# A hybrid decoder layer: the low weights of gate and up 64 bytes further in their tile, the mixers' later tiles realigned, a diagonal moved into a token tile

## The chip, the cores and the metric

One core of a Trainium2 chip runs the whole layer as one program. The metric is the device time of one execution in microseconds (us). The kernel before takes 1016.15 us (median of three runs, 1015.79 to 1016.25).

## The reference

All values are float32, the sequence has 256 tokens, the model width D is 2048, the feed-forward width 5632.

```python
h = rms_norm(x, g_mix)
z_pool, z_q, z_kv, z_kr, z_mq = split(h @ w_in)
y = concat(pool_mixer(z_pool), mla_mixer(z_q, z_kv, z_kr), memory_cross_attention(z_mq, mem))
x = x + y @ w_o
h = rms_norm(x, g_ffn)
g, u = h @ w_gate, h @ w_up                 # 2048 x 5632 each
gc = conv_b + sum(conv_w[j] * shift(g, j))  # causal, width 3, along tokens
x = x + (silu(gc) * u) @ w_down
```

The weights are streamed once from HBM, about 190 MB, and each is used for 256 tokens.

## The kernel before

**Two parts for each number.** A product is made of rounded fp32 parts (the type is called fp32r). Each loaded weight tile `wr` (128 partitions x 2048 columns) is cut by `split_w` (L92) into a high part `wh`, cast by ScalarE (L98), and a low part `wl`, the difference, by VectorE (L99), 1024 columns at a time. `wr`, `wh` and `wl` have three buffers each. Activations have such a pair too, stored side by side: 256 columns of the high part and 256 of the low part. What is computed is high x high, high weight x low activation and low weight x high activation.

**Two ways round.** TensorE (PE) multiplies a stationary operand, 128x128, which a LDWEIGHTS brings in (PEld in the profile), by a moving operand that is streamed past it.

- `gemm_t` (L103), used for gate, up and the input projections, takes the *weights* as stationary. For eight blocks of 128 input features it issues eight products with `wh`, each moving all 512 columns of the activation (both parts at once), and eight with `wl`, each moving the 256 columns of the high part. The order is high, low, low, high, so that sixteen high products stand in a row, then sixteen low ones. Line L116 is both, told apart by the names `h,wh` and `h,wl` (`h` is `h2`, the normalized input of the feed-forward part) or `xg,wh` and `xg,wl` (the input projections).
- `gemm_n` (L122), used for the latent up-projections, the memory's keys and values and the output projection, takes the *activation* as stationary (`mg`, `xg`, `zl`, `cat`, `catm`) and moves 512 columns of `wh` (L134, L135) and `wl` (L136). The down projection does the same (L832 to L834) with the activations `aT` and `aS`.

**Stages by time in the profile.** Memory keys and values to 51 us, queries and rope keys to 78 us, input projections and latent up-projections (stationary `zl`) to 179 us, the output projection (stationary `cat`, and `catm` for the memory heads, with attention heads between) to 290 us, gate and up to 782 us (44 blocks, for each a gate tile and an up tile of 1 MB), the down projection to the end.

**Where things lie.** SBUF addresses are given out in the order of allocation and are fixed when the program is built. In the program before, `wr`, `wh`, `wl`, `h2`, `mg`, `xg`, `cat` and `aT` all begin 64 bytes past a multiple of 128. `gqk` (L311) is 8 bytes wide, and what the mixers allocate behind it (`rot`, `kr`, `tok`, `catm`, `zl`, `p` and others) begins 96 bytes past a multiple of 128, so 32 bytes off from the rest. The blocks of 128 columns inside these tiles are 512 bytes long, so every stationary block keeps its tile's offset.

**The diagonal.** `x1_rstd` (L739) puts the reciprocal root of the mean square on a diagonal `dg` (L743) and multiplies by ones (L745), which gives it as a row for all partitions, `r1`. `dg` has a constant tile of 1024 bytes. `tok` is a tag with three buffers for short-lived token-major tiles in the mixers' pool, which is released after `x1_rstd`; the feed-forward tiles (`g`, `gc`, `u`, `aT`, `aS`) are then put at the same place.

The order within an engine is mostly decided by a scheduler from priorities and dependences; `keep` fixes it by hand in places.

Of the kernel before, what the change touches and what calls it, by code (L numbers as in the profile page):

```python
# [11 lines left out]
F32 = mybir.dt.float32  # L12
F32R = mybir.dt.float32r
# [5 lines left out]
P = 128  # L19
# [41 lines left out]
def layer(ctx, tc, xT_d, xn_d, memT_d, vec_d, tab_d, w_z_d, w_mqkr_d, w_q_d, w_kv_d, w_mem_d, w_pool_d, w_o_d,  # L61
# [10 lines left out]
    def nm(s):  # L72
        uid[0] += 1
        return f"{s}_{uid[0]}"
# [14 lines left out]

        return tc.keep_in_program_order(ins) if on else ins  # L90

    def split_w(raw, o, n, cut=HS, kept=False):  # L92

        hi = stage.tile([P, HS], F32R, tag="wh", name=nm("wh"), bufs=3)
        lo = stage.tile([P, HS], F32R, tag="wl", name=nm("wl"), bufs=3)
        for c in range(0, n, cut):
            e = min(n, c + cut)
            keep(nc.scalar.copy(hi[:, c:e], raw[:, o + c:o + e]), kept)  # L98
            keep(nc.vector.tensor_tensor(lo[:, c:e], raw[:, o + c:o + e], hi[:, c:e].bitcast(F32), op=ALU.subtract),  # L99
                 kept)  # L100
        return hi, lo

    def gemm_t(ps, raw, o, act, ks, first=True, last=True, kept=False, between=None):  # L103


        ks = list(ks)
        nk = HS // P
        cs = range(0, len(ks), nk)
        for c in cs:
            kc = ks[c:c + nk]  # L110
            hi, lo = split_w(raw, o + c * P, len(kc) * P)

            for low in ((False, True) if c // nk % 2 == 0 else (True, False)):
                for i, k in enumerate(kc):
                    w = (lo if low else hi)[:, i * P:(i + 1) * P]
                    keep(nc.tensor.matmul(ps[:, T if low else 0:2 * T], w, act(k)[:, 0:T] if low else act(k),  # L116
                                          start=first and c + i == 0 and not low,
                                          stop=last and c == cs[-1] and i == len(kc) - 1 and low == (c // nk % 2 == 0),
                                          skip_group_check=True), kept)
            if between is not None and c == 0:  # L120
                between()

    def gemm_n(pss, hi, lo, act, k0, first, last, kept=False):

        nk, n = hi.shape[1], hi.shape[2]
        nj = len(pss[0])
        w = n // nj
        for i in range(nk):
            for tt in range(NT):
                xh = act[:, k0 + i, tt * P:(tt + 1) * P]  # L130
                xl = act[:, k0 + i, T + tt * P:T + (tt + 1) * P]
                for j in range(nj):
                    ps, o = pss[tt][j], slice(j * w, (j + 1) * w)
                    keep(nc.tensor.matmul(ps, xh, hi[:, i, o], start=first and i == 0, stop=False), kept)  # L134
                    keep(nc.tensor.matmul(ps, xl, hi[:, i, o], start=False, stop=False), kept)  # L135
                    keep(nc.tensor.matmul(ps, xh, lo[:, i, o], start=False, stop=last and i == nk - 1), kept)  # L136
# [34 lines left out]
    def rsqrt_(dst, src, scale):  # L171

        nc.scalar.activation(dst, src, AF.Sqrt, bias=eps[:], scale=scale)
        nc.vector.reciprocal(dst, dst)
# [96 lines left out]
    for c in range(KD // 2):  # L271
        raw = raw0 if c == 0 else load_w(w_mem_d[c], STG)
        if 0 < c < KD // 2 - 1:
            nc.sync.dma_start(xT[:, 2 * c + 2:2 * c + 4, :], memT_d[:, 2 * c + 2:2 * c + 4, :])
        for i in range(2):
            k = 2 * c + i
            mem_parts(k, k + 1)
            hi, lo = split_w(raw, i * HS, HS, 512 if c == 0 else HS, True)
            gemm_n(pss, hi[:].unsqueeze(1), lo[:].unsqueeze(1), mg, k, k == 0, k == KD - 1)
        if c % 2:  # L280
            h = slice(2 * c - 2, 2 * c + 2)
            ms.add(xT[:, h, :])
            nc.gpsimd.dma_start(xT[:, h, :], xT_d[:, h, :])
        if c in (4, 6):
            x_parts(2 * c - 8, 2 * c - 4)
# [22 lines left out]
    tab = mp.tile([P, NTAB], F32, name="tab")  # L308
    nc.sync.dma_start(tab[:], tab_d)

    gqk = mp.tile([P, 2], F32, name="gqk")  # L311
    keep(nc.vector.tensor_tensor(gqk[:, 0:1], v("gq_nope"), v("gk_nope"), op=ALU.mult))
    keep(nc.vector.tensor_tensor(gqk[:, 1:2], v("g_q_x"), v("g_k_x"), op=ALU.mult))
    rot = mp.tile([P, 2, NT, 4, 32], F32, name="rot")
# [236 lines left out]
    def q_up(n):  # L551
        raw = load_w(w_q_d[n], STG)
        pss = [[ps_main()[:]] for _ in range(NT)]
        for i in range(2):
            hi, lo = split_w(raw, i * HS, HS)
            gemm_n(pss, hi[:].rearrange("p (k n) -> p k n", n=512), lo[:].rearrange("p (k n) -> p k n", n=512),
                   zl, 2 * i, i == 0, i == 1)
        for tt in range(NT):
            ps = pss[tt][0]
            t = tok()  # L560
            if n < 2:
                nc.scalar.copy(t[:], ps)
                head_sq(ssq_n[:, tt, 4 * n:4 * n + 4], t[:].rearrange("p (h d) -> p h d", d=NOPE))
                to_features(qnT[:, 4 * n:4 * n + 4], t, tt, 4, gqk[:, 0:1])
            else:
                t1 = tok()
                nc.scalar.copy(t1[:], ps)
                p3 = t1[:].rearrange("p (h d) -> p h d", d=ROPE)
                head_sq(ssq_r[:, tt, :], p3)
                rotate(t[:].rearrange("p (h d) -> p h d", d=ROPE), p3, 0, tt, H)  # L570
                to_features(qrT, t, tt, 4)
# [9 lines left out]
    def kv_up(n):  # L581
        raw = load_w(w_kv_d[n], STG)
        for h in range(2):
            pss = [[ps_main()[:]] for _ in range(NT)]
            hi, lo = split_w(raw, h * HS, HS)
            gemm_n(pss, hi[:].rearrange("p (k n) -> p k n", n=512), lo[:].rearrange("p (k n) -> p k n", n=512),
                   zl, 4, True, True)
            for tt in range(NT):
                ps = pss[tt][0]
                p3 = ps.rearrange("p (h d) -> p h d", d=128)  # L590
                if n == 1:
                    nc.scalar.activation(vv[:, tt, 4 * h:4 * h + 4, :], p3, AF.Copy, scale=skv[:, tt:tt + 1])
                    continue
                t = tok()
                t3 = t[:].rearrange("p (h d) -> p h d", d=NOPE)
                o = slice(tt * H + 4 * h, tt * H + 4 * h + 4)
                nc.scalar.copy(t[:], ps)
                head_sq(fk[:, o], t3)
                nc.vector.tensor_scalar(fk[:, o], fk[:, o], skv2[:, tt:tt + 1], sskr[:, tt:tt + 1],
                                        op0=ALU.mult, op1=ALU.add)  # L600
                rsqrt_(fk[:, o], fk[:, o], 1.0 / QK)
                nc.vector.tensor_scalar(fkn[:, o], fk[:, o], skv[:, tt:tt + 1], None, op0=ALU.mult)
                nc.vector.tensor_scalar(fkr[:, o], fk[:, o], rx[:, tt:tt + 1], None, op0=ALU.mult)
                nc.vector.tensor_tensor(t3, t3, fkn[:, o].unsqueeze(2).to_broadcast([P, 4, NOPE]), op=ALU.mult)
                to_features(knT[:, 4 * h:4 * h + 4], t, tt, 4, None, "v")
# [73 lines left out]
    def out_part(i, n, pss, c):  # L679

        raw = load_w(w_o_d[i, n, c], STG)
        for h in range(2):
            hi, lo = split_w(raw, h * HS, HS)
            w = [t[:].rearrange("p (k n) -> p k n", n=NN) for t in (hi, lo)]
            k = c * 4 + h * 2
            act, k = (cat, 4 + k) if i else (cat, k) if k < 4 else (catm, k - 4)
            for r in range(2):
                kept = i == 0 or n + c == 0
                gemm_n(pss, *(t[:, r:r + 1] for t in w), act, k + r, c + h + r == 0, c + h + r == 3, kept)
                if kept:  # L690
                    mla_steps()
# [42 lines left out]

    rc = const.tile([P, NT], F32, name="rc")
    r1 = const.tile([P, T], F32, name="r1")
    dg = const.tile([P, T], F32, name="dg")

    def x1_rstd():  # L739
        nc.vector.tensor_reduce(rc[:], ssx[:], axis=AX.X, op=ALU.add)  # L740
        rsqrt_(rc[:], rc[:], 1.0 / D)
        for tt in range(NT):
            nc.vector.tensor_scalar(dg[:, tt * P:(tt + 1) * P], identf[:], rc[:, tt:tt + 1], None, op0=ALU.mult)  # L743
        ps = ps_aux()
        nc.tensor.matmul(ps[:, 0:T], ones[:], dg[:], start=True, stop=True)  # L745
        nc.scalar.copy(r1[:], ps[:, 0:T])


# [56 lines left out]
    for f in range(1, KF):  # L805
        pss = []
        for w in (w_g_d, w_u_d):
            raw = load_w(w[f], STG)
            pss.append(ps_main())
            gemm_t(pss[-1], raw, 0, lambda k: h2[:, k, :], range(KD))  # L810
        glu(f, *pss)


# [190 lines left out]
```

## Time and profile before

| | |
|---|---|
| median of the runs | 1016.15 us |
| profiled execution, its time | 1015.66 us |
| profiled execution, its span | 1013.9 us |
| granted TensorE clock, mean | 0.999 |
| busy: PE, PEld, DVE, ACT | 99%, 86%, 74%, 57% of the span |
| read from HBM | 195 MB, 197 GB/s over the span |

The span is the time from the first to the last instruction; 1.8 us of the execution's time lies around it. PE is busy nearly throughout, so a group's line in the profile (how many, mean duration of one) says less than the distance between the starts of two products that follow each other, here called the **pitch**. A product's recorded duration contains the way through the array and overlaps the next one's; the pitch is what a row of products costs. It is read from the timeline, where equal instructions that follow each other are merged into a row with their first start and their count.

### The profile page before, as it was taken

The page shows a single profiled execution, that of the slowest core. Times are in us where ns is not written, and L with a number is a line of the kernel's source. Part 1 is how long each engine was busy: PE and PEld are TensorE (multiplying, and loading weights), DVE is VectorE, ACT ScalarE, POOL GpSimd, SP SyncE. Part 2 cuts the span into 40 slices and gives each one's busy share as a digit, 9 for nine tenths or more (in the row PEclk, how much of TensorE's full clock was granted, in tenths as well). Part 3 has the DMA queues.
Part 4 walks back from the last instruction along what each step waited for, and adds up shares of the span by engine and source line. Part 5 has one row for each costly group of instructions (what it writes and reads, how often), then busy time and mean ns, then how long its engine had stood idle before and what let it go on. Part 6 is the DMA issues. An engine that isn't in the chain of part 4 may idle for free.

```text
span 1013.9 us, 14132 instructions
## 1 busy us (share of the span) xinstructions
PE 1008.2 (99%) x5356; PEld 868.6 (86%) x5356; DVE 752.4 (74%) x1134; ACT 577.5 (57%) x853; POOL 18.5 (2%) x39
## 2 busy tenths in 40 slices
PE   9999999999999999999999999999999999999998
PEld 7898888888888888888888888888888888888886
DVE  6878689855677676777767676776767788888886
ACT  6678666544576555555545555554655555545653
POOL 1010000000000000000000000000000000010000
PEclk9999999999999999999999999999999999999999
DMA  9777344344665555555555555555545765575561
GB/s 337 278 252 286 130 162 177 130 143 144 210 206 207 181 193 192 183 201 176 197 180 203 178 196 190 185 187 190 205 170 207 256 217 194 208 284 210 208 208 42
DMA packets 31476, 200.17 MB, mean 197 GB/s; under 512 B 3632, under 2 KB 4144, under 8 KB 9392
## 3 DMA queue, kind: packets, MB, share of 16 engines
q1 hardware_dynamic: 28368, 189.44, 52.8%
q0 software_dynamic: 2752, 9.44, 2.6%
q8 instruction: 42, 0.69, 0.3%
q10 hardware_dynamic: 288, 0.38, 0.1%
q14 instruction: 26, 0.21, 0.1%
HBM read 195.06 MB, written 4.19 MB: 197 GB/s over the span
## 4 chain that ended last, share of the span: by engine, by line
PE 99%; DMA 0%; SPq 0%; DVE 0%; ACT 0%; issue 0%
PE psm L116 54%; PE psm L134 5%; PE psm L136 5%; PE psm L135 5%; PE psm L834 4%; PE psa L834 4%; PE psm L833 4%; PE psa L832 4%; PE psa L833 4%; PE psm L832 4%; PE psa L653 1%; PE psa L134 1%; PE psa L136 1%; PE psa L135 1%; PE psa L232 1%; PE psa L429 1%
## 5 line engine op out<-in xcount | busy, mean ns | idle before, releaser
L99 DVE TENSOR_TENSOR wl<-wr,wh 128x1024 fp32r<-128x1024 f32 (+2 forms) x338 | 392.4, 1165 | 65.4 <-ACT wh L98 59.7
L98 ACT CAST wh<-wr 128x1024 fp32r<-128x1024 f32 (+2 forms) x338 | 338.8, 1004 | 138.3 <-PE psm L135 48.6
L116 PE MATMUL psm<-h,wh 128*128 128x512 f32 x1408 | 336.9, 391 | 0.0
L116 PEld LDWEIGHTS psm<-h,wh 128*128 128x128 f32 x1408 | 258.5, 188 | 49.9
L116 PEld LDWEIGHTS psm<-h,wl 128*128 128x128 f32 x1408 | 180.8, 191 | 7.0
L116 PE MATMUL psm<-h,wl 128*128 128x256 f32 x1408 | 182.9, 283 | 0.0
L99 DVE TENSOR_TENSOR wl<-dn,wh 128x1024 fp32r<-128x1024 f32 x58 | 67.8, 1221 | 26.3 <-ACT wh L98 26.3
L98 ACT CAST wh<-dn 128x1024 fp32r<-128x1024 f32 x58 | 59.2, 1052 | 38.3 <-PE psm L833 21.7
L758 ACT COPY g<-psm 128x256 f32<-128x256 f32 x44 | 16.4, 374 | 91.3 <-PE psm L116 91.2
L759 DVE TENSOR_TENSOR g<-g,psm 128x256 f32<-128x256 f32 x44 | 18.5, 420 | 61.0 <-ACT g L758 61.0
L759 DVE TENSOR_TENSOR u<-u,psm 128x256 f32<-128x256 f32 x44 | 18.5, 421 | 55.6 <-ACT u L758 55.6
L769 ACT ACTIVATE gc<-gc 128x256 f32<-128x256 f32 x44 | 18.4, 418 | 63.8 <-DVE gc L768 63.7
L768 DVE SCALAR_TENSOR_TENSOR gc<-g,vec,gc 128x255 f32<-128x255 f32 x88 | 42.1, 478 | 0.3
L832 PE MATMUL psa<-wh,aT 128*128 128x512 f32 x104 | 40.5, 389 | 0.0
L833 PE MATMUL psa<-wh,aT 128*128 128x512 f32 x104 | 40.5, 389 | 0.0
L834 PE MATMUL psa<-wl,aT 128*128 128x512 f32 x104 | 40.5, 389 | 0.0
L832 PE MATMUL psm<-wh,aT 128*128 128x512 f32 x104 | 40.5, 389 | 0.0
L833 PE MATMUL psm<-wh,aT 128*128 128x512 f32 x104 | 40.5, 389 | 0.0
L834 PE MATMUL psm<-wl,aT 128*128 128x512 f32 x104 | 40.5, 389 | 0.0
L116 PE MATMUL psm<-xg,wh 128*128 128x512 f32 x160 | 40.0, 394 | 0.0
L134 PE MATMUL psm<-wh,cat 128*128 128x512 f32 x96 | 38.2, 398 | 0.0
L136 PE MATMUL psm<-wl,cat 128*128 128x512 f32 x96 | 37.5, 390 | 0.0
(227 smaller groups left out, 1394.6 us busy)
## 6 DMA issues: line engine op xcount, KB each, us to landing
wr<-in_w_g SPq DMA_DIRECT2D x44, 1024.0 KB, 4.8
wr<-in_w_u SPq DMA_DIRECT2D x44, 1024.0 KB, 4.8
wr<-in_w_dn SPq DMA_DIRECT2D x33, 1024.0 KB, 4.8
wr<-in_w_o SPq DMA_DIRECT2D x16, 1024.0 KB, 4.9
dn<-in_w_dn SPq DMA_DIRECT2D x11, 1024.0 KB, 4.8
wr<-in_w_z SPq DMA_DIRECT2D x10, 1024.0 KB, 5.7
wr<-in_w_mem SPq DMA_DIRECT2D x7, 1024.0 KB, 7.9
wr<-in_w_mqkr SPq DMA_DIRECT2D x8, 576.0 KB, 4.1
```

The costliest lines, as they stand in the source:

```text
L98: keep(nc.scalar.copy(hi[:, c:e], raw[:, o + c:o + e]), kept)
L99: keep(nc.vector.tensor_tensor(lo[:, c:e], raw[:, o + c:o + e], hi[:, c:e].bitcast(F32), op=ALU.subtract), kept)
L116: keep(nc.tensor.matmul(ps[:, T if low else 0:2 * T], w, act(k)[:, 0:T] if low else act(k), start=first and c + i == 0 and not low, stop=l ...
L134: keep(nc.tensor.matmul(ps, xh, hi[:, i, o], start=first and i == 0, stop=False), kept)
L135: keep(nc.tensor.matmul(ps, xl, hi[:, i, o], start=False, stop=False), kept)
L136: keep(nc.tensor.matmul(ps, xh, lo[:, i, o], start=False, stop=last and i == nk - 1), kept)
L759: nc.vector.tensor_tensor(t[:], t[:], ps[:, T:2 * T], op=ALU.add)
L768: nc.vector.scalar_tensor_tensor(gc[:, d:T], g[:, 0:T - d], v(w, f), gc[:, d:T], op0=ALU.mult, op1=ALU.add)
L769: nc.scalar.activation(gc[:], gc[:], AF.Silu)
L832: nc.tensor.matmul(ps, a[0], b[0], start=first, stop=False)
L833: nc.tensor.matmul(ps, a[1], b[0], start=False, stop=False)
L834: nc.tensor.matmul(ps, a[0], b[1], start=False, stop=last)
```

## The change

- `split_w` allocates the low tile 32 columns (128 bytes) wider and returns a window of it that begins `shift` columns in. `gemm_t` passes `shift` on. Only the gate and up blocks from the second on ask for 16 columns (64 bytes); everywhere else it is 0.
- `gqk` becomes 128 bytes wide.
- `dg` is no constant tile any more, and takes a buffer of `tok`.

```diff
-    def split_w(raw, o, n, cut=HS, kept=False):
+    def split_w(raw, o, n, cut=HS, kept=False, shift=0):
         hi = stage.tile([P, HS], F32R, tag="wh", name=nm("wh"), bufs=3)
-        lo = stage.tile([P, HS], F32R, tag="wl", name=nm("wl"), bufs=3)
+        lo = stage.tile([P, HS + 32], F32R, tag="wl", name=nm("wl"), bufs=3)[:, shift:shift + HS]
...
-    def gemm_t(ps, raw, o, act, ks, first=True, last=True, kept=False, between=None):
+    def gemm_t(ps, raw, o, act, ks, first=True, last=True, kept=False, between=None, shift=0):
...
-            hi, lo = split_w(raw, o + c * P, len(kc) * P)
+            hi, lo = split_w(raw, o + c * P, len(kc) * P, shift=shift)
...
-    gqk = mp.tile([P, 2], F32, name="gqk")
+    gqk = mp.tile([P, 32], F32, name="gqk")
...
-    dg = const.tile([P, T], F32, name="dg")
     def x1_rstd():
...
+        dg = tok()
...
-        nc.tensor.matmul(ps[:, 0:T], ones[:], dg[:], start=True, stop=True)
+        nc.tensor.matmul(ps[:, 0:T], ones[:], dg[:, 0:T], start=True, stop=True)
...
-            gemm_t(pss[-1], raw, 0, lambda k: h2[:, k, :], range(KD))
+            gemm_t(pss[-1], raw, 0, lambda k: h2[:, k, :], range(KD), shift=16)
```

No instruction is added, removed or moved: each engine has the same sequence in both programs. What differs are addresses, modulo 128 bytes:

| tile | before | after |
|---|---|---|
| low weights of gate and up, stationary | 64 | 0 |
| all other low weights | 64 | 64 |
| `wr`, `wh`, `h2`, `mg`, `xg`, `cat`, `aT`, `aS` | 64 | 64 |
| `catm`, `zl`, stationary | 96 | 64 |
| `tok`, `rot`, `kr`, `hsq`, `hadd`, `p`, `pT` | 96 | 64 |

In absolute terms `wr` and `wh` move down by 1024 bytes and the activations by 640, so that modulo 256 the activations go from 192 to 64 while `wh` stays at 192. One wait is added: ScalarE's first copy into `g` (L758) also waits for VectorE's writing of the diagonal, since the diagonal now lies in the released pool.

More of the change, by code (lines that the diff above doesn't have):

```diff
@@ L278, in layer @@
             hi, lo = split_w(raw, i * HS, HS, 512 if c == 0 else HS, True)
-            gemm_n(pss, hi[:].unsqueeze(1), lo[:].unsqueeze(1), mg, k, k == 0, k == KD - 1)
+            gemm_n(pss, hi[:].unsqueeze(1), lo.unsqueeze(1), mg, k, k == 0, k == KD - 1)
         if c % 2:
@@ L555, in q_up @@
             hi, lo = split_w(raw, i * HS, HS)
-            gemm_n(pss, hi[:].rearrange("p (k n) -> p k n", n=512), lo[:].rearrange("p (k n) -> p k n", n=512),
+            gemm_n(pss, hi[:].rearrange("p (k n) -> p k n", n=512), lo.rearrange("p (k n) -> p k n", n=512),
                    zl, 2 * i, i == 0, i == 1)
@@ L585, in kv_up @@
             hi, lo = split_w(raw, h * HS, HS)
-            gemm_n(pss, hi[:].rearrange("p (k n) -> p k n", n=512), lo[:].rearrange("p (k n) -> p k n", n=512),
+            gemm_n(pss, hi[:].rearrange("p (k n) -> p k n", n=512), lo.rearrange("p (k n) -> p k n", n=512),
                    zl, 4, True, True)
@@ L683, in out_part @@
             hi, lo = split_w(raw, h * HS, HS)
-            w = [t[:].rearrange("p (k n) -> p k n", n=NN) for t in (hi, lo)]
+            w = [t.rearrange("p (k n) -> p k n", n=NN) for t in (hi[:], lo)]
             k = c * 4 + h * 2
```

## The prediction

> **What bounds the kernel now.** First the page's busy line and its chain.
>
> ```profile
> PE 1008.2 (99%) x5356; PEld 868.6 (86%) x5356; DVE 752.4 (74%) x1134; ACT 577.5 (57%) x853; POOL 18.5 (2%) x39
> PE 99%; DMA 0%; SPq 0%; DVE 0%; ACT 0%; issue 0%
> PE psm L116 54%; PE psm L134 5%; PE psm L136 5%; PE psm L135 5%; PE psm L834 4%; PE psa L834 4%; PE psm L833 4%; PE psa L832 4%; PE psa L833 4%; PE psm L832 4%; PE psa L653 1%; PE psa L134 1%; PE psa L136 1%; PE psa L135 1%; PE psa L232 1%; PE psa L429 1%
> ```
>
> The chain that ends last is TensorE alone, more than half of it in line 116. So the time is the sum of pitches of matmuls, and an edit that changes only addresses can act only by changing a pitch. Next the stage where line 116 lives, gate and up (columns: stretch, its length, busy us and count of PE, PEld, DVE, ACT, POOL, granted clock, DMA share, GB/s).
>
> ```profile
> 291.00:782.00 491.00, 491.00 (x2826) 433.65 (x2825) 350.09 (x520) 273.28 (x400) 0.54 (x1) 1.00 0.54 190
> ```
>
> PE has no gap in 491 us at full clock; VectorE has 141 us to spare, ScalarE 218 us, the DMA engines nearly half. Then the timeline of PE inside it.
>
> ```profile
> 500.11 2.08 PE L116 MATMUL psm<-h,wl 128*128 128x256 f32 x16
> 502.02 3.82 PE L116 MATMUL psm<-h,wh 128*128 128x512 f32 x16
> 505.67 2.08 PE L116 MATMUL psm<-h,wl 128*128 128x256 f32 x16
> 507.59 3.82 PE L116 MATMUL psm<-h,wh 128*128 128x512 f32 x16
> 511.24 2.08 PE L116 MATMUL psm<-h,wl 128*128 128x256 f32 x16
> ```
>
> A run of sixteen high products takes 505.67 - 502.02 = 3.65 us, a pitch of 228 ns; a run of sixteen low ones takes 507.59 - 505.67 = 1.92 us, a pitch of **120 ns**. The low product moves half the columns and costs more than half. Why, the next rows say: what the load and the multiply of each kind take (min/median/max in ns, then the span of starts).
>
> ```profile
> L116 PEld LDWEIGHTS psm<-h,wh x1408: 186/188/192, 290.6 to 781.7; 128*128 128x128 f32 x176
> L116 PEld LDWEIGHTS psm<-h,wl x1408: 187/192/192, 292.3 to 780.1; 128*128 128x128 f32 x176
> ...
> L116 PEld LDWEIGHTS psm<-h,wh 128*128 128x128 f32 x1408 | 258.5, 188 | 49.9
> L116 PEld LDWEIGHTS psm<-h,wl 128*128 128x128 f32 x1408 | 180.8, 191 | 7.0
> ```
>
> The loads of low weights stand at 192 ns, the top of their range, and the loader is idle before them for 7.0 us in all, against 49.9 us before the high ones. In a low run the loads are queued without pause: the load, not the stream of 256 columns, sets the 120 ns.
>
> **The change part by part.** No instruction is added, removed or moved. There are three effects of address.
>
> *The mixers' stationary blocks, from 96 to 64 modulo 128.* The output projection alternates between `catm` (at 96) and `cat` (at 64), with the same moving weights. This is a comparison that the kernel makes itself.
>
> ```profile
> 210.07 0.40 PE L134 MATMUL psm<-wh,catm 128*128 128x512 f32 x1
> ...
> 212.17 0.39 PE L134 MATMUL psm<-wh,cat 128*128 128x512 f32 x1
> ...
> 212.63 0.39 PE L136 MATMUL psm<-wl,cat 128*128 128x512 f32 x1
> ...
> 213.99 0.39 PE L136 MATMUL psm<-wl,cat 128*128 128x512 f32 x1
> ```
>
> From 210.07 to 212.17 there are nine products of `catm`: 233 ns each. From 212.63 to 213.99 there are six of `cat`: 227 ns each. So an offset of 32 bytes costs 6 ns a product, although the load is hidden behind 512 moving columns. This is the row on which everything else leans: the address of the stationary block reaches the pitch. How many such products there are:
>
> ```profile
> L135 PE MATMUL psm<-wh,zl 128*128 128x512 f32 x40 | 16.3, 406 | 0.0
> L134 PE MATMUL psm<-wh,catm 128*128 128x512 f32 x32 | 13.0, 406 | 0.0
> ```
>
> Three lines each, so 3 x 40 + 3 x 32 = 216 products; after the change they stand as `cat` does, and 216 x 6 ns = **1.3 us** goes. All of it lies on PE, which ends the chain. Its bounds: nothing, if other engines' waits in these stages take it back, and 2 us with the handovers between `catm` and `cat`.
>
> *The low weights of gate and up, from 64 to 0.* The trace has no stationary block at 0, so this is bounded from both sides. The lower end is a load at its fastest. The attention scores load a 128x128 fp32 block for each product, and move 128 columns at a slower rate:
>
> ```profile
> 184.17 0.38 PE L653 MATMUL psa<-qkv 128*128 128x128 f32 x2
> 184.39 0.39 PE L653 MATMUL psa<-qkv,mqT 128*128 128x128 f32 x2
> 184.61 0.22 PE L653 MATMUL psa<-cmask,identb 128*128 128x128 bf16 x1
> ```
>
> Four products in 0.44 us: 110 ns, load included. So a load of this size can be 10 ns quicker than in a low run, and what differs there is that the moving operand is read more slowly. I read the excess as the load and the moving read getting in each other's way, by addresses. That the first step of a run is shorter agrees; the same run from two windows, at its first and its second product:
>
> ```profile
> 500.11 0.28 PE L116 MATMUL psm<-h,wl 128*128 128x256 f32 x1
> 500.22 0.40 PE L116 MATMUL psm<-h,wl 128*128 128x256 f32 x2
> ```
>
> That step is 0.11 us: 256 moving columns alone do not ask for 120 ns. The upper end is 120 + 6 = 126 ns, if 64 bytes off act as 32 bytes off did on `catm`. Between 110 and 126 the trace doesn't decide. I take **115 ns**, halfway from 120 to the lower end and a little above that first step, its nearest row, since in a low run a quicker load shortens the pitch at once: 1408 x 5 ns = **7.0 us**. The Trainium skill has a rule here, in "TensorE: Matmul & The Clock Gate", section "Back-to-back issue gap": 256 columns need 262 cycles warm, 109 ns. The rows differ from it (120 ns here, and 227 ns where it has 216 ns for 512 columns); if the change brought the low products to the rule, an estimate from that page would be 1408 x 11 = 15.5 us.
>
> *Everything else that slid.* Modulo 256 the activations move by 128 bytes against `wh`, which touches all high products and the down projection. The query projection already has both cases: its moving halves of 288 columns begin at 64 and 192 modulo 256 in turn.
>
> ```profile
> 59.89 0.29 PE L134 MATMUL psa<-wh,xg 128*128 128x288 f32 x1
> ...
> 60.29 0.29 PE L134 MATMUL psa<-wh,xg 128*128 128x288 f32 x1
> ...
> 60.69 0.29 PE L134 MATMUL psa<-wh,xg 128*128 128x288 f32 x1
> ```
>
> Three products take 0.40 us in either half, 133 ns each: 128 bytes make no difference, and I cost it at nothing. VectorE writes the low tile at a new offset; 176 splits share its 141 us to spare, 0.8 us each, which hides a slower write. The diagonal in `tok` and the added wait cost nothing:
>
> ```profile
> 295.38 0.48 DVE L743 TENSOR_SCALAR dg<-identf,rc 128x128 f32<-128x128 f32 x2
> ...
> 301.81 0.38 ACT L758 COPY g<-psm 128x256 f32<-128x256 f32 x1
> ```
>
> The copy into `g`, with ScalarE's later casts queued behind it, now also waits for a write that ended six microseconds earlier.
>
> *The sum.* 1015.66 (the profiled execution) - 7.0 - 1.3 = 1007.3 us. That execution is 0.49 us below the median of the runs, so 1007.8 us. When the low run shortens by 80 ns, what is late next would be the splits that feed it; with VectorE at 350 of 491 us and the transfers at 54% they have room even at 110 ns.
>
> **The rivals.**
>
> *Nothing changes at the low weights.* The pitch stays at 120 ns because the pattern repeats every 64 bytes, or because the loads are slow for a reason other than address. For it: 0 and 128 bytes behave alike, and if the period is 64 then 64 does as well; and the high product keeps its 227 ns in all of `mg`, `cat` and `aT`. Against it: nothing shows that the period is 64 rather than 128. It leaves the mixers' 1.3 us: 1014.9 us. The Trainium skill would go further, in "SBUF — State Buffer", section "Who interferes with whom": PE has two independent read ports and never waits on anyone. By that rule addresses do nothing at all; the nine rows of `catm` speak against it.
>
> *The low weights get worse.* The load and the moving read now meet more often, in all 1408 low products of line 116, as they do 32 bytes off. For it: the one known departure from the common offset made products slower, and the load in a low run has no cover, so each nanosecond counts in full. At 126 ns it costs 1408 x 6 = 8.4 us, with the mixers' gain 1023.3 us; at 123 ns, 1019.1 us. It decides from 121 ns on, where it eats the 1.3 us; slower by over 0.2% (2.0 us) begins at 122.4 ns. Against it: the high products also had slower rows when a run's rhythm was broken, so 32 bytes may be bad for not fitting a rhythm rather than for being away from 64.
>
> *The gain is given back.* PE runs ahead and waits for casts or weights instead. The shares above speak against it; it would end between the first two cases, near 1012 us.
>
> **How the numbers follow.** The low pitch falls, to 110 to 118 ns: 0.45, 1002 (1408 x 10 = 14.1 us less would be 1000.7 at the very end) to 1012 us, with 1007.8 as its middle. Nothing at the low weights: 0.31, 1013.5 to 1016.3 us. Worse: 0.19, 1017 to 1023 us. Given back: 0.05. A difference of 0.2%, 2.0 us, is about what a measurement of this kernel can tell from no change. Faster by more than that is the first and the last case: 0.50; within it 0.31; slower 0.19. A range from 1001.5 to 1019.5 us leaves out the fastest end of the first case (some 0.04) and the upper half of the slower one (some 0.10).
>
> **What would show it.** In the changed kernel's timeline the sixteen low products of gate and up: a run of 1.84 us is my 115 ns, 1.92 us is the first rival, 2.0 us the second. The loads of `h,wl` should fall from a median of 192 ns if they stop being queued. The products of `zl` and `catm` should stand 227 ns apart; 233 ns would refute the first term. High runs should stay at 3.65 us; if they move, addresses modulo 256 matter after all, and my third item is wrong. Idle time of PE in gate and up, none now, would mean the gain was given back.

## The result, and the profile after

The changed kernel takes 1024.86 us (median of five runs, 1024.26 to 1028.07), the kernel before 1016.25 us beside it (five runs, 1015.79 to 1019.15): a ratio of **1.0092, 95% interval 1.0079 to 1.0105**. It is 0.9% slower where 0.8% faster was forecast.

First the page's span, its busy line and the shares of the chain that ended last, of the changed kernel.

```profile
span 1026.3 us, 14132 instructions
...
PE 1018.7 (99%) x5356; PEld 868.3 (85%) x5356; DVE 754.8 (74%) x1134; ACT 578.6 (56%) x853; POOL 18.5 (2%) x39
...
PE 98%; DMA 1%; SPq 0%; DVE 0%; ACT 0%; issue 0%
```

PE is still the whole chain but for one per cent of DMA, with the same 5356 products: it is busy 10.5 us longer on the same work. The profiled execution is the slowest of the five (1028.07 us); part of what it has over the median is in the first stage, where PE's waits name the same two waits as before, and one of them is longer (columns: us in total, times, longest):

```profile
PE psm L134 <- ACT wh L98: 2.5, 2, 2.2
PE psa L169 <- DVE eps L162: 1.1, 1, 1.1
```

The first of them was 0.6 us before. Right behind it the granted clock is low for some three microseconds, where it was 1.00 in the same stretch before (columns as in the prediction):

```profile
12.00:15.00 3.00, 2.78 (x7) 2.16 (x8) 1.69 (x3) 2.06 (x5) 0.00 (x0) 0.56 0.86 333
```

Nine products take 3.75 us there, 12.22 to 15.97 in the timeline, for some 2.1 us at their usual pitch. Of the 12.4 us between the two profiled executions, then, 1.9 are that wait and 1.7 that clock, together about what this execution has over the median. So the comparison goes by pitches and by stages, not by the two spans. Gate and up in the windows (columns as in the prediction):

```profile
290.00:791.00 501.00, 501.00 (x2863) 437.02 (x2862) 355.83 (x525) 278.49 (x405) 1.08 (x2) 1.00 0.53 189
```

There is no gap in PE there, at full clock, with the other engines as idle as before. Nothing was handed to a wait. The timeline of PE in that stretch says where the time is:

```profile
501.22 2.01 PE L116 MATMUL psm<-h,wl 128*128 128x256 f32 x16
503.07 3.88 PE L116 MATMUL psm<-h,wh 128*128 128x512 f32 x16
506.78 2.05 PE L116 MATMUL psm<-h,wl 128*128 128x256 f32 x16
508.67 3.67 PE L116 MATMUL psm<-h,wh 128*128 128x512 f32 x15
```

A low run takes 503.07 - 501.22 = 1.85 us, or 1.89 the next time, where it took 1.92: the low products did get quicker. A high run takes 506.78 - 503.07 = 3.71 us where it took 3.65: the high products, whose weights the change does not touch, got slower. The groups of line 116 agree, from the page (busy us, mean ns of one, idle before):

```profile
L116 PE MATMUL psm<-h,wh 128*128 128x512 f32 x1408 | 342.6, 395 | 0.0
L116 PEld LDWEIGHTS psm<-h,wh 128*128 128x128 f32 x1408 | 258.5, 188 | 54.5
L116 PEld LDWEIGHTS psm<-h,wl 128*128 128x128 f32 x1408 | 177.8, 188 | 7.8
```

The low loads fell from a mean of 191 ns to 188, as they should if they queue less; but the high products rose (391 ns before). The down projection, of which the diff changes not one line, shows the same. Before, then after (min/median/max ns, span of starts):

```profile
L832 PE MATMUL psa<-wh,aT x104: 389/389/389, 782.2 to 895.3; 128*128 128x512 f32 x104
```

```profile
L833 PE MATMUL psa<-wh,aT x104: 388/392/404, 790.3 to 905.6; 128*128 128x512 f32 x104
L835 PE MATMUL psm<-wl,aT x104: 388/392/404, 906.8 to 1021.9; 128*128 128x512 f32 x104
```

The first group's starts spread over 113.1 us before and 115.3 after; a duration that was 389 ns for every one of them now varies from 388 to 404.

From here on pitches are means over the whole trace: the distance from one product's start to the next, of all that are under 300 ns (so that a wait at a stage's edge doesn't count), sorted by operand; the last column is their count after the change.

| 512 columns, ns | before | after | pitches |
|---|---|---|---|
| high, gate and up (`h2`) | 228.4 | 232.5 | 1404 |
| down (`aT`) | 226.7 | 231.1 | 623 |
| down (`aS`) | 227.7 | 231.8 | 378 |
| output projection (`cat`) | 227.7 | 231.4 | 279 |
| memory (`mg`) | 226.9 | 231.4 | 177 |
| input projections, high (`xg`) | 229.7 | 233.7 | 156 |
| `catm` | 233.0 | 230.0 | 92 |
| `zl` | 233.5 | 230.0 | 112 |
| **256 columns: low, gate and up** | 119.5 | 117.2 | 1408 |

Every kind of 512-column product that slid by 128 bytes against its weights lost some 4 ns. The three kinds whose own offset the edits set, `zl`, `catm` and the low products, gained 2.3 to 3.5 ns.

### The profile page after: what moved, and what is told of

Same layout as the page of the kernel before. It is cut to its first block, busy times and chain, and to the rows that moved or that the text cites. A ratio compares the mean times of both kernels' runs of the same rounds, so it can differ in the third digit from the quotient of the medians.

```text
span 1026.3 us, 14132 instructions
## 1 busy us (share of the span) xinstructions
PE 1018.7 (99%) x5356; PEld 868.3 (85%) x5356; DVE 754.8 (74%) x1134; ACT 578.6 (56%) x853; POOL 18.5 (2%) x39
## 4 chain that ended last, share of the span: by engine, by line
PE 98%; DMA 1%; SPq 0%; DVE 0%; ACT 0%; issue 0%
PE psm L116 53%; PE psm L134 5%; PE psm L135 5%; PE psm L136 5%; PE psm L834 4%; PE psm L833 4%; PE psa L834 4%; PE psa L833 4%; PE psm L835 4%; PE psa L835 4%; PE psa L654 1%; PE psa L134 1%; PE psa L136 1%; PE psa L135 1%; DMA wr<-in_w_mem 1%; PE psa L232 1%
## 5 line engine op out<-in xcount | busy, mean ns | idle before, releaser
L116 PE MATMUL psm<-h,wh 128*128 128x512 f32 x1408 | 342.6, 395 | 0.0
L116 PEld LDWEIGHTS psm<-h,wl 128*128 128x128 f32 x1408 | 177.8, 188 | 7.8
L116 PE MATMUL psm<-h,wl 128*128 128x256 f32 x1408 | 179.7, 279 | 0.0
L134 PE MATMUL psm<-wh,cat 128*128 128x512 f32 x96 | 38.6, 402 | 0.0
L135 PE MATMUL psm<-wh,cat 128*128 128x512 f32 x96 | 37.8, 393 | 0.0
```

## The experiments

Three theories. **A**: the pitch of a 512-column product depends on the distance between the addresses of its moving and its stationary operand, modulo 256 bytes; the slide by 128 bytes took that distance from nothing to 128. **B**: the shift of the low weights itself slows the high products that follow, and other stages for a reason of their own. **C**: the place of the activations alone counts, whatever the weights do. The edits are against the changed kernel, if nothing else is said. Each run's ratio is against the kernel before on the same chip (medians 1016.05 to 1016.24 us, 14 to 25 runs).

**The slide undone, the shift kept.** With a low tile 256 bytes wider instead of 128, the activations keep their distance from `wh`.

```diff
-        lo = stage.tile([P, HS + 32], F32R, tag="wl", name=nm("wl"), bufs=3)[:, shift:shift + HS]
+        lo = stage.tile([P, HS + 64], F32R, tag="wl", name=nm("wl"), bufs=3)[:, shift:shift + HS]
```

> The low tile is padded by 256 bytes and not 128, so that behind its three buffers the activations lie where they lay before against the high weights modulo 256; the shift of the low weights by 64 bytes stays. Theory A (the pitch of a product follows the difference of moving and stationary address modulo 256, and the slide of 128 bytes made the high products slow): high runs of gate and up back at 3.65 us for sixteen, down projection back at 227 ns, low pitch near 115 ns, about 1009 us. Theory B (the shift of the low weights itself made the high products slow, the slide is harmless): high runs stay near 3.72 us, about 1020 to 1024 us.

Measured: 1013.46 us, ratio 0.9976 (0.9966 to 0.9985). PE's timeline in gate and up, and the down projection's last line:

```profile
501.46 3.81 PE L116 MATMUL psm<-h,wh 128*128 128x512 f32 x16
505.11 2.05 PE L116 MATMUL psm<-h,wl 128*128 128x256 f32 x16
507.00 3.81 PE L116 MATMUL psm<-h,wh 128*128 128x512 f32 x16
```

```profile
L835 PE MATMUL psm<-wl,aT x104: 388/389/390, 894.5 to 1007.6; 128*128 128x512 f32 x104
```

High runs are back at 3.65 us, `aT` back at 389 ns and 113.1 us, and the low run stays at 1.89 us. B falls: the shift is there and the high products don't mind. The three wider buffers put the activations 768 bytes further from `wh` than in the kernel before, and that costs nothing where 128 bytes cost 4 ns: a period of 256 bytes fits, one of 128 doesn't. The size was missed, 1013.46 us for about 1009: the low pitch is 117.9 ns, not the 115 that I still expected.

**The slide alone.** The reverse: the wider tile and the freed constant tile stay, the shift and the wider `gqk` go.

```diff
-            gemm_t(pss[-1], raw, 0, lambda k: h2[:, k, :], range(KD), shift=16)
+            gemm_t(pss[-1], raw, 0, lambda k: h2[:, k, :], range(KD), shift=0)
...
-    gqk = mp.tile([P, 32], F32, name="gqk")
+    gqk = mp.tile([P, 2], F32, name="gqk")
```

> The changed kernel without the shift of the low weights and with the narrow gqk: what is left is the low tile padded by 128 bytes, the diagonal in a token tile, and so the slide of the activations by 128 bytes modulo 256. Theory A: about 1026 us, high runs of gate and up near 3.72 us, the products of the down projection near 231 ns. Theory B: 1016 us as before, 3.65 us and 227 ns.

Measured: 1029.19 us, ratio 1.0127 (1.0110 to 1.0144). The same two views:

```profile
501.33 2.08 PE L116 MATMUL psm<-h,wl 128*128 128x256 f32 x16
503.25 3.88 PE L116 MATMUL psm<-h,wh 128*128 128x512 f32 x16
506.96 2.06 PE L116 MATMUL psm<-h,wl 128*128 128x256 f32 x16
```

```profile
L833 PE MATMUL psa<-wh,aT x104: 388/392/404, 792.6 to 908.0; 128*128 128x512 f32 x104
```

Low run 1.92 us as before the change, high run 3.71, `aT` over 115.4 us. The slide without any intended part of the change is slower than the change itself.

**Neither slide nor shift.** The 256-byte tile with a shift of 0, and `gqk` at 128 bytes as in the change.

```diff
-        lo = stage.tile([P, HS + 32], F32R, tag="wl", name=nm("wl"), bufs=3)[:, shift:shift + HS]
+        lo = stage.tile([P, HS + 64], F32R, tag="wl", name=nm("wl"), bufs=3)[:, shift:shift + HS]
...
-            gemm_t(pss[-1], raw, 0, lambda k: h2[:, k, :], range(KD), shift=16)
+            gemm_t(pss[-1], raw, 0, lambda k: h2[:, k, :], range(KD), shift=0)
```

> As e1_pad256, without the shift. Both theories: as the kernel before, 1015.5 to 1016.5 us, low pitch 120 ns, high runs 3.65 us; catm and zl now at a difference of 128 bytes, so under theory A still 232 ns a product instead of 233. If it is off from the kernel before by more than 2 us, the diagonal's new place or the padding matters by itself.

Measured: 1015.93 us, ratio 1.0002 (0.9992 to 1.0011): the time of before. It prices the two halves. Against the slide alone, **the slide costs 1029.19 - 1015.93 = 13.3 us**. From the pitches of these two runs: high 1404 x 4.4 = 6.2, `aT` 623 x 4.4 = 2.7, `aS` 378 x 4.1 = 1.6, the other 512-column rows of the table 2.6 us, 13.1 together. Against the first run, which has the shift too, **the shift gains 1015.93 - 1013.46 = 2.5 us**, and 1408 x 1.6 ns is 2.3.

It also holds a miss of mine that the times can't show. `zl` and `catm` lie here 128 bytes off `wh` modulo 256, that is, aligned modulo 128 as I had wanted them, and they stand at 233.0 and 232.2 ns, as in the program before (233.5 and 233.0). By the pitches the wider `gqk` bought some 0.1 us of the 1.3.

**All of them at no distance.** By A, `zl` and `catm` need another 128 bytes.

```diff
-        lo = stage.tile([P, HS + 32], F32R, tag="wl", name=nm("wl"), bufs=3)[:, shift:shift + HS]
+        lo = stage.tile([P, HS + 64], F32R, tag="wl", name=nm("wl"), bufs=3)[:, shift:shift + HS]
...
-    gqk = mp.tile([P, 32], F32, name="gqk")
+    gqk = mp.tile([P, 64], F32, name="gqk")
```

> As e1_pad256, with gqk 256 bytes wide, so that catm and zl lie as the other activations do modulo 256. Theory A: the products of catm and zl at 227 ns, 1.3 us below e1_pad256, about 1008 us. Theory B: no more than 1 us below e1_pad256, above 1018 us.

Measured: 1012.73 us, ratio 0.9969 (0.9957 to 0.9980). `catm` is at 227.6 ns, `zl` at 228.8. In the output projection, PE's timeline:

```profile
209.99 0.39 PE L136 MATMUL psm<-wl,catm 128*128 128x512 f32 x1
...
212.04 0.39 PE L136 MATMUL psm<-wl,catm 128*128 128x512 f32 x1
...
214.08 0.39 PE L136 MATMUL psm<-wl,cat 128*128 128x512 f32 x1
```

Nine products of `catm` take 2.05 us and nine mostly of `cat` 2.04: 228 and 227 ns, no difference left. By the pitches that is 92 x 4.6 + 112 x 4.3 = 0.9 us against the kernel with the slide undone; by the medians 0.7 us, which these intervals alone don't tell from nothing; the total of about 1008 us that I expected still had the low products at 115 ns in it. This kernel beats both the one before and the changed one.

**Weights and activations slid together.** C says that the place of the activations counts, A that only the distance does. To the kernel *before*, one constant tile of 128 bytes is added that nothing reads, ahead of all of them, with a memset of one element.

```diff
+    skip = const.tile([P, 32], F32, name="skip")
+    nc.vector.memset(skip[:, 0:1], 0.0)
```

> The kernel before with 128 bytes of unused constant tile in front, so that weights and activations slide together by 128 bytes modulo 256 and every difference stays. If the difference of moving and stationary address sets the pitch (theory A): 1016 us, high runs 3.65 us, down projection 227 ns. If the place of the activations alone does (theory C: an operand at 64 modulo 256 is slow, whatever the other is): about 1026 us, 231 ns in the down projection.

Measured: 1015.82 us, ratio 0.9998 (0.9989 to 1.0008); high 228.4 ns, `aT` 226.7, low 119.5. The timeline in gate and up:

```profile
501.77 3.82 PE L116 MATMUL psm<-h,wh 128*128 128x512 f32 x16
505.43 2.08 PE L116 MATMUL psm<-h,wl 128*128 128x256 f32 x16
507.34 3.82 PE L116 MATMUL psm<-h,wh 128*128 128x512 f32 x16
```

3.66 and 1.91 us: the same slide of the activations, with the weights along, costs nothing. C falls.

**Another distance: 64 bytes.** The slide alone again, with a low tile that is 64 bytes wider: three buffers make 192 bytes, modulo 256 a distance of 64 the other way.

```diff
-        lo = stage.tile([P, HS + 32], F32R, tag="wl", name=nm("wl"), bufs=3)[:, shift:shift + HS]
+        lo = stage.tile([P, HS + 16], F32R, tag="wl", name=nm("wl"), bufs=3)[:, shift:shift + HS]
...
-    gqk = mp.tile([P, 32], F32, name="gqk")
+    gqk = mp.tile([P, 2], F32, name="gqk")
...
-            gemm_t(pss[-1], raw, 0, lambda k: h2[:, k, :], range(KD), shift=16)
+            gemm_t(pss[-1], raw, 0, lambda k: h2[:, k, :], range(KD), shift=0)
```

> As e2_slide_only with the low tile padded by 64 bytes and not 128, so that the activations stand 64 bytes and not 128 off the high weights modulo 256. A dose of the slide. Theory A with a period of 256: the down projection's products between 227 and 235 ns; if the cost grows with the distance from 0, 229 ns and about 1021 us; if any distance costs the same, 231 to 233 ns and about 1027 us. Theory C: 227 ns, 1016 us, since nothing lies at 64 any more.

Measured: 1024.88 us, ratio 1.0086 (1.0071 to 1.0101). The 512-column products are at 232.9 (`h2`), 231.0 (`aT`) and 231.1 ns (`aS`), as at 128 bytes; the total is 4.3 us smaller than that of the slide alone, 3.1 of it because the low products gain, at 117.3 ns: the pads put the low weights off their activations too. So the cost does not grow with the distance. With the 32 bytes of `zl` and `catm` in the program before (233 ns) there are three distances, and each costs 3 to 6 ns; `zl` and `catm` in the slide alone, 160 bytes off `wh`, make a fourth, at 233.5 and 233.2 ns. The timeline has both kinds, and behind it three of the 288-column products of the query projection in the same kernel:

```profile
505.35 3.89 PE L116 MATMUL psm<-h,wh 128*128 128x512 f32 x16
509.09 2.03 PE L116 MATMUL psm<-h,wl 128*128 128x256 f32 x16
```

```profile
60.91 0.30 PE L134 MATMUL psa<-wh,xg 128*128 128x288 f32 x1
61.05 0.29 PE L135 MATMUL psa<-wh,xg 128*128 128x288 f32 x1
61.18 0.29 PE L136 MATMUL psa<-wl,xg 128*128 128x288 f32 x1
61.31 0.29 PE L134 MATMUL psa<-wh,xg 128*128 128x288 f32 x1
```

A high run is 509.09 - 505.35 = 3.74 us. The 288-column products take 0.40 us for three, 133 ns, what they took before the change and after it, though here neither half of `wh` stands at distance 0; the means over the trace, for the products that move `wh`, are 133.9 ns here and 134.7 before and after. **The 512-column product answers to the distance and the 288-column product doesn't.**

**How far the low weights should stand.** Four further shifts on the kernels without the slide: 128 and 192 bytes with `gqk` at 128 bytes, 32 and 96 with `gqk` at 256. The shift is the only number in which the four differ from those kernels; in floats it is 32, 48, 8 and 24, for instance:

```diff
-            gemm_t(pss[-1], raw, 0, lambda k: h2[:, k, :], range(KD), shift=16)
+            gemm_t(pss[-1], raw, 0, lambda k: h2[:, k, :], range(KD), shift=32)
```

> As e1_pad256 with the low weights shifted by 128 bytes and not 64. If the low pitch falls with any distance from the moving operand: 117 ns or less, 1013 us. If 64 is special and 128 acts as it does on the high products: 120 ns or more, 1016 us or more.

> As e1_pad256 with the low weights shifted by 192 bytes and not 64, which is 64 on the other side modulo 256. If the sign of the distance doesn't matter: 118 ns and 1013.5 us as e1_pad256; if it does: another low pitch, between 113 and 122 ns, so 1007 to 1020 us.

> As e8_all256 with the low weights shifted by 32 bytes and not 64. On the high products 32 bytes (catm and zl before), 64 and 128 bytes cost about alike; on the low ones 64 bytes won 1.6 ns and 128 nothing. If the gain of the low products needs the full 64 bytes: 119 to 122 ns, 1014.5 us or more. If it comes with any distance below 128: 118 ns, 1012.7 us as e8_all256.

> As e8_all256 with the low weights shifted by 96 bytes. By the same two readings: 119 to 122 ns and 1014.5 us or more, or 118 ns and 1012.7 us.

Measured, with the kernels above for 0 and 64 (the last two columns are gate and up from first to last, and the ratio; the times of 32 and 96 include the 0.7 us or so of `zl` and `catm`):

| low weights from `h2`, bytes | low, ns | high beside them, ns | gate and up, us | median, us | ratio |
|---|---|---|---|---|---|
| 0 | 119.5 | 228.4 | 491.6 | 1015.93 | 1.0002 (0.9992 to 1.0011) |
| 32 | 118.2 | 230.1 | 492.1 | 1015.63 | 0.9995 (0.9985 to 1.0005) |
| 64 | 117.9 | 228.4 | 489.3 | 1013.46 | 0.9976 (0.9966 to 0.9985) |
| 96 | 117.4 | 228.5 | 488.7 | 1012.47 | 0.9965 (0.9949 to 0.9981) |
| 128 | 120.2 | 227.7 | 491.6 | 1015.83 | 0.9997 (0.9988 to 1.0006) |
| 192 | 117.8 | 230.6 | 492.2 | 1016.42 | 1.0006 (0.9997 to 1.0015) |

At 128 bytes the low products gain nothing, and at 96 they gain what they gain at 64, each as one of the two readings had it. At 32 and 192 bytes the low pitch of 118 ns came without the time that was expected with it: the high products beside them, whose own operands did not move, lose a little more than the low ones gain: with 192 the timeline has 3.69 us for a high run,

```profile
502.83 3.85 PE L116 MATMUL psm<-h,wh 128*128 128x512 f32 x16
506.52 2.05 PE L116 MATMUL psm<-h,wl 128*128 128x256 f32 x16
508.40 3.85 PE L116 MATMUL psm<-h,wh 128*128 128x512 f32 x16
```

and with 96 it has 3.66 and 1.87:

```profile
501.33 3.82 PE L116 MATMUL psm<-h,wh 128*128 128x512 f32 x16
504.99 2.04 PE L116 MATMUL psm<-h,wl 128*128 128x256 f32 x16
506.86 3.82 PE L116 MATMUL psm<-h,wh 128*128 128x512 f32 x16
```

So B wasn't empty: where the low weights stand can reach their neighbours, at 32 and 192 bytes though not at 64, 96 or 128, and by 2 ns rather than 4. The traces tell this effect from that of the slide, if the high pitches are sorted by their place in the run of sixteen (means over 85 runs). With the low weights at 64 bytes, and likewise in the kernel before with them at 0, the first five places have 228 to 236 ns and the rest 227: a run-in. At 32 bytes the run-in is nine places long, at 192 ten, at 128 two, and behind it stand 227 ns again, up to the fifteenth place or the last. In the slide alone and in the changed kernel the high products never get there: 229 to 237 ns at all sixteen places. No rule for the length of the run-in came out of these six distances. The best two, 96 bytes at 1012.47 us and 64 bytes with everything aligned at 1012.73, are not told apart.

In the changed kernel itself the low weights don't stand at 64 bytes throughout. Against `wh`, the pads of 128 bytes put its three buffers of `wl` 0, 128 and 256 bytes further along and `h2` 384, so with the shift of 64 they stand 192, 64 and 192 bytes from `h2`, modulo 256.

## Why the prediction was wrong

**What bounds the kernel** was right: PE alone, by the sum of its pitches, and only a pitch could change. So was that no other engine would take a gain back: PE has no gap in 501 us after the change either, and the diagonal's move shows nowhere in PE's waits; the longer wait in the first stage is on `wh`, far ahead of it.

**The failed step is the third item, "Everything else that slid": "128 bytes make no difference, and I cost it at nothing."** It is worth +12.5 us. The slide touches all 512-column products but those of `zl` and `catm`: with the differences of the table above, 1404 x 4.1 = 5.8 us in gate and up, 623 x 4.4 + 378 x 4.1 = 4.3 us in the down projection, 279 x 3.7 + 177 x 4.5 + 156 x 4.0 = 2.5 us in the stages ahead of them. I had the right suspicion and tested it on the wrong rows: the three of the query projection have 288 columns, and that product is the one that doesn't answer. The 512-column rows that did carry the answer were quoted in the same prediction, for the first item: `catm` against `cat`, 32 bytes, 6 ns. I took them for a matter of alignment within 128 bytes. They were the first case of any distance at all, as the 64 and 128 bytes of the experiments showed: what counts is the distance between the two operands modulo 256, not the offset of either modulo 128. What I wrote under what would show it, high runs that leave 3.65 us, is what happened.

**The low weights** had the right sign, and the forecast was twice the size: 119.5 to 117.2 ns, 1408 x 2.3 = 3.2 us for 7.0. The lower end of 110 ns came from a product of another kind, and the short first step of a run may only say what a run could do whose loads are already in. The sign was in part luck. I reckoned with the offset of the weights alone, modulo 128; the low products are quicker where the weights stand *off* the moving operand by 32, 64, 96 or 192 bytes and not at 0 or at 128, and nothing that I had told 64 bytes from 128. At distance 0 they are slow, the reverse of what holds for 512 columns. Whether load and moving read get in each other's way, as I read it, stays open. The Trainium skill's rule in "TensorE: Matmul & The Clock Gate", section "Back-to-back issue gap", would have given 109 ns for 256 columns. No mean over a trace here, of the low products of gate and up, came below 117.2.

**The mixers' blocks** gained half of the 1.3 us: 92 x 3.0 + 112 x 3.5 = 0.7 us. They reach distance 0 to `wh` only because the slide of 128 bytes came on top of the wider `gqk`, and the pad leaves one of the three buffers of `wl` 128 bytes off the other two. Sorted by buffer, `catm` times `wl` in that buffer stands at 232.7 ns and `wh` beside it at 231.9, in the other two at 229.1 to 229.9 and 227.6 to 229.3. For `cat`, which lies where that buffer does, it is the other way round: 228.9 ns with that `wl`, 232.0 and 233.0 with the others. So theory A can be read inside one program, too. PE's timeline has the slow and the quick kind one after the other:

```profile
208.95 0.40 PE L134 MATMUL psm<-wh,catm 128*128 128x512 f32 x1
...
211.51 0.40 PE L136 MATMUL psm<-wl,catm 128*128 128x512 f32 x1
...
214.49 0.39 PE L135 MATMUL psm<-wh,catm 128*128 128x512 f32 x1
...
216.78 0.40 PE L136 MATMUL psm<-wl,catm 128*128 128x512 f32 x1
```

Eleven steps in 2.56 us, 233 ns, with the buffer that is off; ten in 2.29 us, 229 ns, with another.

**The sum** by measured terms: -3.2 - 0.7 + 12.5 = +8.6 us on 1016.25, 1024.9 us, against a median of 1024.86. All of the miss is accounted for: 12.5 from the slide, 3.8 from the low weights, 0.6 from the mixers, 17 us between forecast and result.

**The rivals.** None is what happened. "The low weights get worse" has the sign, and its place is wrong: they got better. "Nothing changes at the low weights" is refuted by their loads and by the 2.5 us of the shift alone. "The gain is given back" would have shown as idle time of PE in gate and up, and there is none. Two programs that differ in nothing but start addresses, the slide alone and the one with neither slide nor shift, are 13.3 us apart, 13.1 of it in PE's pitches. So what I drew from the rule of the Trainium skill's "SBUF — State Buffer", section "Who interferes with whom", by which PE's two read ports are independent and PE waits on no one, doesn't hold for these products: addresses do act.

**What stays open**: the mechanism. That 512 columns lose at every distance tried but 0, 288 columns don't, and 256 columns gain at some, fits a meeting of the load's reads with the stream's at regular times, but nothing here shows the reads, and no other width was tried.

## What to carry to other kernels

Where PE has no gaps, an allocation is an edit: padding one tile moves every tile behind it, so list the start addresses of both operands of each large group of products, before and after, modulo 256, and look at their difference rather than at either one. Pad in steps of 256 bytes, so that only what is meant to move moves; here that alone turned a loss of 0.9% into a gain of 0.2 to 0.3%. And price a change by rows of the same shape as what it touches: a row that shows no effect for another shape is no evidence of none.

## What the runs showed of the hardware

- 512 moving columns of fp32r with a weight load for each product: 227 to 230 ns, by stage, when both operands start at the same address modulo 256 bytes, 231 to 234 ns at a distance of 32, 64, 128 or 160. Moving both together changes nothing (ratio 0.9998, 0.9989 to 1.0008).
- 288 columns: 133 ns in the rows shown, 134 to 135 as the mean over a trace for those that move `wh`, whose two halves stand at 0 and 128 or at 64 and 192.
- 256 columns, in gate and up: 119.5 to 120.2 ns at 0 and 128 bytes, 117.4 to 118.2 at 32, 64, 96 and 192, and at 32 and 192 the 512-column products beside them lose 1.7 and 2.2 ns, by a longer run-in at the start of each run.
